# Taking the norm's row scale out of the transposes: weights at the split, roots at the products

## The chip, the cores and the metric

The kernel runs on one core of a Trainium2 chip. The metric is device time in microseconds (us), the median of three runs. One more execution was recorded by the profiler; every row below is from it.

## The reference

512 tokens of 1024 features pass through two blocks. Only the first block is touched. It is, cut to what matters:

```python
def rms_norm(x, g):
    y = x * rsqrt(mean(x * x, axis=-1) + EPS)
    return y * g

h = rms_norm(x, g_mix_norm)
z = h @ w_in        # q, k | v, o | gates | c_q, c_kv | k_pe
...                 # mLSTM heads from q, k, v, o, gates; latent attention from c_q, c_kv, k_pe
x = x + concat(y_a, y_b) @ w_out
h = rms_norm(x, g_ffn_norm)
x = x + square(relu(h @ w_ff1)) @ w_ff2
```

A norm multiplies row t of x by a root r(t), and column k by a weight g(k). r(t) goes through a product with a matrix unchanged, so it may be applied before or after it. The second block (retention, differential attention, PEER) has norms of its own.

## The kernel before

**Tiles.** The tokens are 4 blocks of 128 rows (`tb`). A matrix product contracts over features, so both operands must have features on the partitions: the normed activations are kept transposed, as `xTh` and `xTl` (128 features x 8 feature tiles x 512 tokens). A float32 number is held as a rounded high part and the rest, and one product is three TensorE matmuls (`mm3`, L130 to L132: high by high, high by low, low by high). A weight page of 128x1024 is loaded into one of three buffers `raw`, then split by ScalarE (`Ah`, L105) and VectorE (`Al`, L86; GpSimd for the very first page).

**The norm before.** For each block: ScalarE squares the row and sums it (L164), VectorE adds EPS (`rsqt`, L137), GpSimd takes the power -1/2 (`r`, L138), VectorE forms `hn` = x * r * g (L172; g was loaded as a 512 KB tile `gb` that repeats it on all partitions). TensorE transposes the eight 128x128 tiles of `hn` into two PSUM banks (`ptr`, L156), and for each bank ScalarE writes the high part of all four tiles in one instruction (L159, 128x512) and VectorE the low part in another (L86). Products then come out as the reference has them.

**First use, at the start.** `ws_first` multiplies three pages of `w_in` (gates, then two of the latent pages) by the transposed tokens in two halves of 256 tokens: 3 pages x 8 tiles x 3 matmuls for the first half, the transposes of the last blocks, then the second half. After it come the gate rows (`F7`, transposed to `pf` at L375), the latent vectors `ch`, `cl` and `csq` from the banks `pw` and `pc` (L417 to L420), the q and kv products `puq`, the normed keys `na` (L509) and their transposes `pqt` (L531), the convolution of `pq` (L594 and on) and the v and o products.

**Second use, at the FFN.** `out_last` adds the product with `w_out` to x block by block (`pol`), and takes one step of the norm after each block; then `ws_first` multiplies the first three pages of `w_ff1`. Relu (ScalarE, L734) and square (VectorE, L735) follow on each of 32 such products. While this runs, weight pages of the second block are split ahead (`shl`, ScalarE L117, GpSimd L86) and written to memory.

**Order.** A scheduler writes the instructions of each engine into one queue; an engine takes its queue in order and waits at the first instruction that isn't ready. Loads are issued by SyncE's queue, each waiting for its buffer. At the start a hand-written stretch (`manual_schedule`) gives the order for ScalarE and VectorE.

## Time and profile before

| | |
|---|---|
| median of three runs | 2127.32 us (2127.05 to 2130.56) |
| the profiled execution: its time | 2128.51 us |
| the profiled execution: its span | 2126.7 us |
| TensorE matmuls busy | 2090.7 us (98%) |
| VectorE, ScalarE, GpSimd busy | 1541.3, 858.6, 534.6 us |

A row of the timeline gives the start in us from the span's start, the duration, the engine (PE is TensorE, DVE VectorE, ACT ScalarE, POOL GpSimd, PEld TensorE's weight load), the line, output<-inputs, shapes, and in brackets how long the engine had been idle and what ended that. A row that groups instructions gives their number, busy time, mean ns of one, and the idle time ahead of them. A row of stretches gives busy us (and instructions) for each engine, then the granted TensorE clock as a share of full speed, the DMA engines' busy share and GB/s.

### The profile page before, as it was taken

To read this page: it belongs to the slowest core of one execution; us is meant where nothing else is said; L and a number is where in the kernel's file an instruction comes from. 1 tells how busy PE (TensorE), PEld (TensorE's weight loads), DVE (VectorE), ACT (ScalarE), POOL (GpSimd) and SP (SyncE) were. 2 spreads that over 40 slices of the span, in tenths; PEclk is the share of its full clock that TensorE was granted. 3 is DMA by queue.
4 is the path that set the end of the run, shared out by engine and by line. 5 is a ranking of instruction groups with operands and counts; after the bars stand their busy time and mean duration, and the time that the engine had idled before them with its cause. 6 is when DMAs were issued, how large, how long until landed. Compare 5 with 4: busy or idle time off the path is not lost.

```text
span 2126.7 us, 29751 instructions
## 1 busy us (share of the span) xinstructions
PE 2090.7 (98%) x10985; PEld 1807.7 (85%) x10985; DVE 1541.3 (72%) x3039; ACT 858.6 (40%) x1505; POOL 534.6 (25%) x387
## 2 busy tenths in 40 slices
PE   7999999999999999999999999999999999999998
PEld 6856888888888778888999999999888889899886
DVE  6846666556444763679979799978888878778784
ACT  5645354444324543311335544333333333333332
POOL 1100034444100000100000004544555554444330
PEclk9999999999999999999999999999999999999999
DMA  5210269899512222354898778999999999998981
GB/s 191 68 41 21 90 239 353 318 340 345 205 60 89 69 70 91 108 199 165 278 352 302 280 228 312 372 360 338 319 343 333 351 319 338 330 335 319 322 291 61
DMA packets 178977, 507.55 MB, mean 239 GB/s; under 512 B 15632, under 2 KB 73872, under 8 KB 172048
## 3 DMA queue, kind: packets, MB, share of 16 engines
q1 hardware_dynamic: 136208, 329.47, 45.6%
q0 software_dynamic: 42624, 176.18, 22.0%
...
## 4 chain that ended last, share of the span: by engine, by line
PE 96%; DVE 1%; DMA 1%; ACT 1%; issue 0%; SPq 0%; POOL 0%; DVEq 0%; POOLq 0%; ACTq 0%
PE pA L130 11%; PE pA L131 11%; PE pA L132 11%; PE po L132 8%; PE po L130 8%; PE po L131 8%; PE pO L131 3%; PE pO L132 3%; PE pO L130 3%; PE pts L132 2%; PE pts L130 2%; PE pts L131 2%; PE pGm L1147 2%; PE pQ L130 1%; PE pQ L131 1%; PE pQ L132 1%
## 5 line engine op out<-in xcount | busy, mean ns | idle before, releaser
L130 PE MATMUL pA<-xTh,Ah 128*128 128x384 f32 (+1 forms) x1256 | 434.0, 346 | 0.3 <-ACT ge L1166 0.3
L132 PE MATMUL pA<-xTh,Al 128*128 128x384 f32 (+1 forms) x1256 | 434.2, 346 | 0.0
L131 PE MATMUL pA<-xTl,Ah 128*128 128x384 f32 (+1 forms) x1256 | 434.0, 346 | 0.0
L105 ACT ACTIVATE Ah<-raw 128x1024 fp32r<-128x1024 f32 x203 | 215.1, 1060 | 329.9 <-PE pA L131 228.2
L86 DVE TENSOR_TENSOR Al<-raw,Ah 128x1024 fp32r<-128x1024 f32 x202 | 249.8, 1237 | 122.7 <-ACT Ah L105 119.1
L1236 POOL DMA_INDIRECT gu<-peer_u_rows,eidx x128 | 182.6, 1426 | 581.0 <-issue 394.3
L132 PE MATMUL po<-Bh,Wl 128*128 128x512 f32 x714 | 278.6, 390 | 0.0
L131 PE MATMUL po<-Bl,Wh 128*128 128x512 f32 x714 | 278.2, 390 | 0.0
L131 PEld LDWEIGHTS pA<-xTl,Ah 128*128 128x128 f32 x1256 | 235.9, 188 | 14.3
L130 PEld LDWEIGHTS pA<-xTh,Ah 128*128 128x128 f32 x1256 | 235.8, 188 | 14.1 <-ACT ge L1166 0.6
L132 PEld LDWEIGHTS pA<-xTh,Al 128*128 128x128 f32 x1256 | 235.8, 188 | 12.0
L1236 POOL DMA_INDIRECT gv<-peer_v,eidx x128 | 190.2, 1486 | 197.2 <-DVE acc L1252 180.2
L130 PE MATMUL po<-Bh,Wh 128*128 128x512 f32 x714 | 225.0, 390 | 0.0
L86 DVE TENSOR_TENSOR Bl<-raw,Bh 128x1024 fp32r<-128x1024 f32 x151 | 193.7, 1284 | 19.9 <-ACT Bh L105 19.2
L1297 ACT ACTIVATE Wh<-w 128x384 fp32r<-128x384 f32 x128 | 67.1, 525 | 342.8 <-PE po L131 313.1
L105 ACT ACTIVATE Bh<-raw 128x1024 fp32r<-128x1024 f32 x151 | 157.7, 1049 | 68.2 <-PE pO L132 45.9
L1252 DVE SCALAR_TENSOR_TENSOR acc<-gv,w,acc 128x1024 f32<-128x1024 f32 x128 | 164.0, 1281 | 2.2 <-DMA gv<-peer_v,eidx 2.2
L1242 DVE SCALAR_TENSOR_TENSOR gu<-gu,hn 128x1024 f32<-128x1024 f32 x128 | 155.8, 1219 | 3.8 <-DMA gu<-peer_u_rows,eidx 3.8
L132 PEld LDWEIGHTS po<-Bh,Wl 128*128 128x128 f32 x714 | 134.0, 188 | 26.2
L86 DVE TENSOR_TENSOR Wl<-w,Wh 128x384 fp32r<-128x384 f32 x128 | 71.1, 556 | 117.4 <-ACT Wh L1297 109.5
L131 PEld LDWEIGHTS po<-Bl,Wh 128*128 128x128 f32 x714 | 134.1, 188 | 25.7
L130 PEld LDWEIGHTS po<-Bh,Wh 128*128 128x128 f32 x714 | 133.2, 188 | 22.1
...
## 6 DMA issues: line engine op xcount, KB each, us to landing
raw<-peer_v SPq DMA_DIRECT2D x128, 512.0 KB, 6.4
raw<-peer_u SPq DMA_DIRECT2D x104, 512.0 KB, 6.5
...
raw<-w_ff SPq DMA_DIRECT2D x64, 512.0 KB, 6.2
...
Al<-Sd SPq DMA_DIRECT2D x40, 512.0 KB, 5.9
Ah<-Sd SPq DMA_DIRECT2D x40, 512.0 KB, 5.5
```

The lines of the kernel that those rows point to most:

```text
L86: eng.tensor_tensor(o, a, hi.bitcast(F32), op=OP.subtract)
L105: S.activation(hi, raw, AF.Copy)
L130: PE.matmul(ps, lh, rh, start=start, stop=False)
L131: PE.matmul(ps, lh, rl, start=False, stop=False)
L132: return PE.matmul(ps, ll, rh, start=False, stop=stop)
L1147: PE.matmul(o, hot[:, 0, jp, :, jb], val[:, p, jp, :, jb], start=p == 0, stop=p == 1)
L1236: G.indirect_dma_start(out=r, out_offset=None, in_=rows, in_offset=bass.IndirectOffsetOnAxis(ap=eidx[s // 64][:, s % 64:s % 64 + 1], axis=0))
L1242: V.scalar_tensor_tensor(r, r, 1.0, xn3, op0=OP.mult, op1=OP.mult, accum_out=act3[:, s:s + 1])
L1252: V.scalar_tensor_tensor(acc3, r, w3[:, s:s + 1], acc3, op0=OP.mult, op1=OP.add)
L1297: S.activation(wh, w, AF.Copy)
```

## The change

Both norms of the first block lose `hn` and `gb`. x itself is transposed. The split of the transposed tile multiplies by g, which is now one number per partition and feature tile: ScalarE writes `xTh` = ptr * g and VectorE `xTl` = ptr * g - `xTh`. As g differs from tile to tile, each bank now takes four ScalarE and four VectorE instructions of 128x128 (L170, L171), where it took one of each. The roots of all four blocks are formed on the side, transposed and copied as `rootT` (the root of token t in column t, on all partitions; L193, L194), and applied where the products are read: as a column of scales where tokens are on the partitions (v, o), by a VectorE multiply with `rootT` where they are on the columns (`F7`, the four `pq`, the FFN's products), and as factors of the small root vectors in the latent part. In the FFN the pair Relu on ScalarE, square on VectorE becomes max-and-multiply on VectorE, square on ScalarE. `hn` rows of blocks 2 and 3 no longer lie in the buffers of `wu`; `kg` shares a buffer now.

```diff
+    def put_raw(h, l, src, kt0, n, tb, gT):
+        pt = bank("att", "ptr")
+        for j in range(n):
+            PE.transpose(pt[:, j * P:(j + 1) * P], src[:, j * P:(j + 1) * P], ident)
+        t = slice(tb * P, (tb + 1) * P)
+        for j in range(n):
+            g, ps = gT[:, kt0 + j:kt0 + j + 1], pt[:, j * P:(j + 1) * P]
+            S.activation(h[:, kt0 + j, t], ps, AF.Copy, scale=g)
+            V.scalar_tensor_tensor(l[:, kt0 + j, t], ps, g, h[:, kt0 + j, t].bitcast(F32), op0=OP.mult, op1=OP.subtract)
...
+        def roots(dst):
+            for tb in range(NT):
+                ss = square_sum(tmp.tile([P, D], F32, tag="hn", name="hn", bufs=2), x[tb])
+                rsq(root[:, tb:tb + 1], ss, 1.0 / D, EPS)
+            pt = bank("att", "prt")
+            for tb in range(NT):
+                PE.transpose(pt[:, tb * P:(tb + 1) * P], root[:, tb:tb + 1].to_broadcast([P, P]), ident)
+            S.activation(dst, pt, AF.Copy)
+            return root
...
-        sq[0]()
-        fin[0]()
-        sq[1]()
-        fin[1]()
         turn[0]()
+        turn[1]()
         pgs.append(page(None, G, raw=raws[0]))
-        sq[2]()
-        turn[1]()
         pgs.append(page(None, V, raw=raws[1]))
-        fin[2]()
-        sq[3]()
-        fin[3]()
+        turn[2]()
         pgs.append(page(None, V, raw=raws[2]))
-        turn[2]()
+    rootT = main.tile([P, D], F32, tag="gb", name="rootT", bufs=1)[:, 0:T]
+    root = roots(rootT)
...
-    S.activation(F7, ps, AF.Identity, bias=gbias)
+    V.tensor_tensor(F7, ps, rootT, op=OP.mult)
+    V.tensor_scalar(F7, F7, gbias, None, op0=OP.add)
...
+    for n, (rc, width) in enumerate(((rcq, 256), (rkv, 128))):
+        c = slice(4 * n, 4 * n + 4)
+        V.tensor_tensor(ssc[:, c], ssc[:, c], root2, op=OP.mult)
+        rsq(rc, ssc[:, c], 1.0 / width, EPS)
+        V.tensor_tensor(rc, rc, root, op=OP.mult)
...
         ws_mm(ps, page(wf[i]), h, l)
+        V.tensor_tensor(ps, ps, rootT, op=OP.mult)
...
-        S.activation(v1[:, tb, :, 0:128], ps.rearrange("p (h d) -> p h d", h=4), AF.Copy)
+        S.activation(v1[:, tb, :, 0:128], ps.rearrange("p (h d) -> p h d", h=4), AF.Copy,
+                     scale=root[:, tb:tb + 1])
...
-        S.activation(og[:, tb], ps, AF.Tanh, scale=0.5)
+        S.activation(og[:, tb], ps, AF.Tanh, scale=half_root[:, tb:tb + 1])
...
+    rootT = fp.tile([P, T], F32, name="rootT")
+    roots(rootT)
...
-            S.activation(r, ps, AF.Relu)
-            V.tensor_tensor(r, r, r, op=OP.mult)
+            V.scalar_tensor_tensor(r, ps, 0.0, rootT, op0=OP.max, op1=OP.mult)
+            S.activation(r, r, AF.Square)
```

How the scheduler lays this out is read from the queues of both programs, below. A row is a place in an engine's queue, the line, output<-inputs, the shape and what it waits for (a counter of PE, DVE, Activation or a DMA queue); xN stands for N such rows in a run.

**ScalarE at the start**, from the first norm instruction to the second weight page, before:

```order
3 L164 ACTIVATE hn,ss<-x 128x1024 [waits DMAHW3_49]
4 L159 ACTIVATE xTh<-ptr 128x4x128 [waits PE_49] x2
5 L105 ACTIVATE Ah<-raw 128x1024 [waits DMAHW4_49]
6 L164 ACTIVATE hn,ss<-x 128x1024 [waits DMAHW5_49]
7 L159 ACTIVATE xTh<-ptr 128x4x128 [waits PE_49] x2
8 L105 ACTIVATE Ah<-raw 128x1024 [waits DMAHW6_49]
```

And now (the stretch between two squares and the second weight page; ahead of it stand seven more `xTh` pieces and three squares):

```order
10 L170 ACTIVATE xTh<-ptr,gT 128x128 [waits DVE_49]
11 L170 ACTIVATE xTh<-ptr,gT 128x128 [waits PE_49]
12 L170 ACTIVATE xTh<-ptr,gT 128x128 [waits DVE_49] x3
13 L170 ACTIVATE xTh<-ptr,gT 128x128 [waits PE_49]
14 L170 ACTIVATE xTh<-ptr,gT 128x128 [waits DVE_49]
15 L194 ACTIVATE rootT<-prt 128x512 [waits PE_49]
16 L170 ACTIVATE xTh<-ptr,gT 128x128 [waits DVE_49]
17 L380 ACT_TABLE_LOAD
18 L380 ACTIVATE sin<-red 128x128 [waits DVE_49]
19 L170 ACTIVATE xTh<-ptr,gT 128x128 [waits DVE_49]
20 L105 ACTIVATE Ah<-raw 128x1024 [waits DMAHW4_49]
21 L105 ACTIVATE Ah<-raw 128x1024 [waits DMAHW6_49]
```

The first weight page moved from behind two `xTh` instructions to behind sixteen, four squares, the copy of the roots and the sine with its table load; and only the first piece of a bank waits for TensorE, the other three wait for VectorE.

**VectorE at the same place**, now (`posf`, `ang`, `nn`, `red` form the rotary angles, `gqk` a product of weights; before, `ang` stood behind all four `xTl` of the first two blocks):

```order
12 L171 SCALAR_TENSOR_TENSOR xTl<-ptr,gT,xTh 128x128 [waits Activation_49] x2
13 L330 TENSOR_SCALAR half_root<-root 128x4 [waits Pool_49]
14 L332 TENSOR_TENSOR root_225<-root 128x4
15 L484 TENSOR_TENSOR gqk<-gq_b,gk_b 128x128 [waits DMAHW6_49,DMAHW5_49]
16 L171 SCALAR_TENSOR_TENSOR xTl<-ptr,gT,xTh 128x128 [waits Activation_49]
17 L362 CAST posf<-posi 128x4 [waits DMAHW0_49]
18 L366 TENSOR_SCALAR ang<-invf,posf 128x32 [waits DMAHW1_49,DVE_49]
19 L171 SCALAR_TENSOR_TENSOR xTl<-ptr,gT,xTh 128x128 [waits Activation_49]
20 L366 TENSOR_SCALAR ang<-invf,posf 128x32 x3
21 L171 SCALAR_TENSOR_TENSOR xTl<-ptr,gT,xTh 128x128 [waits Activation_49]
```

Pieces of the second block now stand behind instructions that wait for the loads of `gq_b`, `gk_b`, `posi` and `invf`; ten pieces stand ahead of `posf`.

**TensorE at the end of the latent stage**, the last transposes of the keys' and queries' parts (`na`, `ro`), before:

```order
442 L132 MATMUL pts<-Ah,xTl 128x512
443 L641 MATMUL pM<-MxP,sel 128x512 x2
444 L536 MATMUL pqt<-ident,ro 128x128 x2
445 L531 MATMUL pqt<-ident,na 128x128 x4
446 L536 MATMUL pqt<-ident,ro 128x128 x2
447 L641 MATMUL pM<-MxP,sel 128x512 x2
448 L531 MATMUL pqt<-ident,na 128x128 x4
449 L536 MATMUL pqt<-ident,ro 128x128 x2
```

And now:

```order
436 L131 MATMUL puq<-hk,ch_539 128x512
437 L132 MATMUL puq<-hk,cl_540 128x512
438 L559 MATMUL pqt<-ident,na 128x128 x4
439 L671 MATMUL pM<-MxP,sel 128x512 x2
440 L564 MATMUL pqt<-ident,ro 128x128 x2
441 L559 MATMUL pqt<-ident,na 128x128 x4
442 L564 MATMUL pqt<-ident,ro 128x128 x2
443 L559 MATMUL pqt<-ident,na 128x128 x4
444 L564 MATMUL pqt<-ident,ro 128x128 x2
```

The products `pts` that stood between the last `puq` and these transposes now stand ahead of the last `puq`, and the first `na` follows it directly.

**ScalarE at the entry of the FFN**, before:

```order
252 L164 ACTIVATE hn,ss<-x 128x1024
253 L159 ACTIVATE xTh<-ptr 128x4x128 x2
254 L117 ACTIVATE shl<-sraw 128x1024
255 L105 ACTIVATE Bh<-raw 128x1024 x2
256 L159 ACTIVATE xTh<-ptr 128x4x128 x2
```

And now:

```order
271 L201 ACTIVATE hn,ss<-x 128x1024
272 L117 ACTIVATE shl<-sraw 128x1024
273 L170 ACTIVATE xTh<-ptr,gT 128x128 x3
274 L117 ACTIVATE shl<-sraw 128x1024
275 L105 ACTIVATE Bh<-raw 128x1024
276 L170 ACTIVATE xTh<-ptr,gT 128x128 x2
277 L105 ACTIVATE Bh<-raw 128x1024
278 L170 ACTIVATE xTh<-ptr,gT 128x128 x6
279 L105 ACTIVATE Bh<-raw 128x1024
280 L170 ACTIVATE xTh<-ptr,gT 128x128 x2
281 L194 ACTIVATE rootT<-prt 128x512
```

The pieces of the last blocks are spread between page splits (`Bh`) and splits ahead (`shl`).

## Rows read from the trace of the kernel before

**Rows 1.** The page: busy us, share of the span and instructions of each engine.
```profile
PE 2090.7 (98%) x10985; PEld 1807.7 (85%) x10985; DVE 1541.3 (72%) x3039; ACT 858.6 (40%) x1505; POOL 534.6 (25%) x387
```

**Rows 2.** Stretches (us): busy us of each engine, granted clock, DMA share, GB/s.
```profile
0.00:13.40 13.40, 3.70 (x16) 3.14 (x16) 4.31 (x10) 7.25 (x11) 4.22 (x10) 1.00 0.85 316
...
44.00:56.00 12.00, 10.15 (x43) 9.04 (x43) 10.29 (x17) 4.28 (x11) 0.00 (x0) 0.72 0.29 89
...
60.00:80.00 20.00, 20.00 (x98) 16.78 (x98) 19.27 (x48) 16.10 (x45) 3.61 (x4) 1.00 0.24 79
...
292.00:296.00 4.00, 2.47 (x11) 2.26 (x11) 4.00 (x4) 1.09 (x2) 0.88 (x2) 0.52 1.02 420
...
640.00:2126.70 1486.70, 1474.04 (x8030) 1309.48 (x8028) 1159.24 (x2368) 559.28 (x950) 385.86 (x273) 1.00 0.74 260
```

**Rows 3.** Timeline of the start: start, duration, engine, instruction, idle time before it.
```profile
4.31 1.06 ACT L164 ACTIVATE hn<-x 128x1024 f32<-128x1024 f32 x1 [2.28 <-DMA x<-x]
...
8.31 1.97 PE L156 MATMUL ptr<-ident,hn 128*128 128x128 f32 x8 [8.31 <-DVE hn L172]
...
10.81 1.05 ACT L105 ACTIVATE Ah<-raw 128x1024 fp32r<-128x1024 f32 x1
...
11.94 2.37 POOL L86 TENSOR_TENSOR Al<-raw,Ah 128x1024 fp32r<-128x1024 f32 x1 [1.64 <-ACT Ah L105]
...
16.04 0.28 PE L131 MATMUL pw<-xTl,Ah 128*128 128x256 f32 x1
...
16.16 0.28 PE L132 MATMUL pw<-xTh,Al 128*128 128x256 f32 x1
...
20.70 0.68 DVE L342 TENSOR_SCALAR ang<-invf,posf 128x32 f32<-128x32 f32 x4 [2.07 <-DMA invf<-c_invf]
...
36.45 0.60 PE L375 MATMUL pf<-ident,F 128*128 128x128 f32 x4
```

**Rows 4.** Groups of ScalarE and VectorE: count, busy us, mean ns, idle before.
```profile
L687 ACT ACTIVATE hf<-pH,dn 128x128 f32<-128x128 f32 x16 | 5.6, 361 | 8.3 <-DVE dn L685 6.2 <-DVE dn L683 1.7 <-DVE dn L684 0.4
...
L688 DVE SCALAR_TENSOR_TENSOR hs<-pH,dn,hf 128x128 f32<-128x128 f32 x16 | 5.5, 345 | 2.1 <-ACT hf L687 1.9
...
L1166 ACT ACT_TABLE_LOAD x6 | 7.7, 1283 | 0.1
...
L668 DVE SCALAR_TENSOR_TENSOR E<-pS,E 128x512 f32<-128x512 f32 x8 | 5.5, 688 | 1.0 <-PE pS L653 0.5 <-ACT E L667 0.5
```

**Rows 5.** Timeline at 45 to 48 us, VectorE, ScalarE and TensorE.
```profile
45.93 0.75 DVE L418 SCALAR_TENSOR_TENSOR cl<-pw,gcq,ch 128x512 fp32r<-128x512 f32 x1
...
46.71 0.60 ACT L420 ACTIVATE csq<-pw 128x512 f32<-128x512 f32 x1 [1.73 <-DVE cl L418]
...
47.36 1.44 PE L426 MATMUL prc<-ones,csq 128*128 128x1 f32 x6 [1.85 <-ACT csq L420]
```

**Rows 6.** DMA issues up to 60 us: count, KB, median us to landing.
```profile
raw<-w_uq SPq DMA_DIRECT2D x2, 512.0 KB, 6.3
```

**Rows 7.** Timeline of the latent stage's end, GpSimd and TensorE.
```profile
112.99 1.01 POOL L138 TENSOR_TENSOR rqk<-rsqt,nhalf 128x4 f32<-128x4 f32 x1 [6.43 <-DVE rsqt L137]
...
115.34 0.63 PE L531 MATMUL pqt<-ident,na 128*128 128x128 f32 x4 [1.43 <-DVE na L509]
```

**Rows 8.** Timeline of the FFN's entry, VectorE, GpSimd, ScalarE, TensorE.
```profile
289.21 4.18 DVE L172 SCALAR_TENSOR_TENSOR hn<-x,r,gb 128x1024 f32<-128x1024 f32 x1 [0.17 <-POOL r L138]
...
289.92 2.37 POOL L86 TENSOR_TENSOR shl<-sraw,shl 128x1024 fp32r<-128x1024 f32 x1
...
286.09 1.04 ACT L164 ACTIVATE hn<-x 128x1024 f32<-128x1024 f32 x1
...
293.53 0.87 PE L156 MATMUL ptr<-ident,hn 128*128 128x128 f32 x3 [3.51 <-DVE hn L172]
...
305.86 0.40 PE L130 MATMUL pA<-xTh,Ah 128*128 128x512 f32 x1
```

More of the change, by code (lines that the diff above doesn't have):

```diff
@@ L160, in put_T, with raw_T, turn, step @@
         sub(V, l[:, kt0:kt0 + n, tb * P:(tb + 1) * P], psv, dst)
+    def put_raw(h, l, src, kt0, n, tb, gT):
[7 more added lines that the diff above has]
+            V.scalar_tensor_tensor(l[:, kt0 + j, t], ps, g, h[:, kt0 + j, t].bitcast(F32), op0=OP.mult, op1=OP.subtract)
+    def raw_T(x, gname, lag=1):
+        gT = main.tile([P, KT], F32, tag="gT", name="gT", bufs=2)
+        nc.sync.dma_start(gT, I[gname])
+        h, l = new_xT()
+        root = main.tile([P, NT], F32, tag="root", name="root", bufs=2)
+        def turn(tb):
+            for half in range(2):
+                put_raw(h, l, x[tb][:, half * 512:(half + 1) * 512], half * 4, 4, tb, gT)
+        def step(tb):
+            if tb >= lag:
+                turn(tb - lag)
+        def roots(dst):
[7 more added lines that the diff above has]
+            return root
+        return h, l, roots, step, [lambda tb=tb: turn(tb) for tb in range(NT)]
     def square_sum(o, xt):
@@ L172, in norm_rows, with norm_T @@
         return V.scalar_tensor_tensor(o, xt, r, gb, op0=OP.mult, op1=OP.mult)
-    def norm_T(x, gname, room=None, lag=1):
+    def norm_T(x, gname, lag=1):
         gb = bcast_row(I[gname], D, "gb")
@@ L192, in step @@
                 done.append(norm_rows(rows[tb], x[tb], gb))
-        if room is None:
-            return h, l, rows, step, [lambda tb=tb: turn(tb) for tb in range(NT - lag, NT)]
-        for tb in range(NT):
-            rows[tb] = room(tb)
-        sums = {}
-        order = [lambda tb=tb: sums.update({tb: square_sum(rows[tb], x[tb])}) for tb in range(NT)]
-        rest = [lambda tb=tb: norm_rows(rows[tb], x[tb], gb, sums[tb]) for tb in range(NT)]
-        turns = [lambda tb=tb: turn(tb) for tb in range(NT)]
-        return h, l, order, rest, turns
+        return h, l, rows, step, [lambda tb=tb: turn(tb) for tb in range(NT - lag, NT)]
     def ws_mm(ps, pg, h, l, n=T):
@@ L279, in body @@
     x = new_x()
+    nc.sync.dma_start(ident, I["c_ident"])
     load_x(x, 0)
-    h, l, sq, fin, turn = norm_T(
-        x, "g_mix_norm",
-        lambda tb: tmp.tile([P, D], F32, tag="hn", name="hn", bufs=2) if tb < 2 else
-        m1.tile([P, 2, D], F32, tag="yb", name="hn", bufs=2)[:, 0])
-    nc.sync.dma_start(ident, I["c_ident"])
+    h, l, roots, _, turn = raw_T(x, "g_mix_norm")
     load_x(x, 1)
@@ L294, in body @@
     with tc.manual_schedule(engines={mybir.EngineType.Activation, mybir.EngineType.DVE}):
-        sq[0]()
-        fin[0]()
-        sq[1]()
-        fin[1]()
         turn[0]()
+        turn[1]()
         pgs.append(page(None, G, raw=raws[0]))
-        sq[2]()
-        turn[1]()
         pgs.append(page(None, V, raw=raws[1]))
-        fin[2]()
-        sq[3]()
-        fin[3]()
+        turn[2]()
         pgs.append(page(None, V, raw=raws[2]))
-        turn[2]()
+    rootT = main.tile([P, D], F32, tag="gb", name="rootT", bufs=1)[:, 0:T]
+    root = roots(rootT)
+    half_root = m1.tile([P, NT], F32, name="half_root")
+    V.tensor_scalar(half_root, root, 0.5, None, op0=OP.mult)
+    root2 = m1.tile([P, NT], F32, name="root2")
+    V.tensor_tensor(root2, root, root, op=OP.mult)
     R = 36
@@ L461, in body @@
         S.activation(sq[:, 0:64], kflat[:, tb], AF.Square, accum_out=ssp[:, tb:tb + 1])
-    kg = lp.tile([P, NT, 64], F32, name="kg")
+    kg = lp.tile([P, NT, 64], F32, tag="ra", name="kg", bufs=1)
     V.tensor_tensor(kg, kflat, gk_b[:, None, 128:192].to_broadcast([P, NT, 64]), op=OP.mult)
@@ L712, in body @@
         sub(V, yl[:, hd, :], pt, yh[:, hd, :])
-    h, l, _, norm, norm_end = norm_T(x, "g_ffn_norm")
+    h, l, roots, norm, norm_end = raw_T(x, "g_ffn_norm")
+    norm_end = norm_end[NT - 1:]
     out_last(x, I["w_out"], yh, yl, lambda: ma.tile([P, T], F32R, tag=f"E{T}", name="X", bufs=4), norm)
@@ L1369, in pack @@
     A["positions"] = np.ascontiguousarray(f("positions").reshape(NT, P).T)
-    for n in ("g_mix_norm", "g_mlstm_out", "g_q", "g_k", "g_ffn_norm"):
+    for n in ("g_mlstm_out", "g_q", "g_k"):
         A[n] = sq(n)
+    for n in ("g_mix_norm", "g_ffn_norm"):
+        A[n] = np.ascontiguousarray(sq(n).reshape(KT, P).T)
     w = sq("w_in")
```

2 lines of the change are left out of this document (removed).

## The prediction

> **What bounds the kernel now.** First the page's busy line: TensorE works in 2090.7 of 2126.7 us [rows 1]. So work taken from the other engines is worth nothing in itself; the time moves where TensorE waits, or by what TensorE is given to do, and that hardly changes (8 transposes of roots more). Next the stretches: from 640 us to the end TensorE is busy in 1474 of 1487 us at full clock [rows 2], the queues there are the same in both kernels, and a delay brought in from before 640 finds nothing to soak it up. All is decided earlier. There the stretches and the timeline show the places where TensorE stands still and the change has a hand: the first 13.4 us, where it is busy for 3.70 [rows 2], 44 to 56 us, the end of the latent stage at 115 us, and the entry of the FFN at 290 us. I take them in turn, as differences at TensorE's next fixed point; a shift of an earlier point is handed on in full since TensorE has no slack in between.
>
> **The pairs.** A bank's split was one ScalarE and one VectorE instruction on 128x512 and is now four of each on 128x128. In the queue each ScalarE piece but the first of a bank waits for a count that VectorE's piece before it in that bank raises, and VectorE's waits for ScalarE's. So in one bank the two take turns. The nearest rows are a pair of the mLSTM stage with the same forms, a 128x128 PSUM read with a scale column on ScalarE, 361 ns, and a 128x128 VectorE instruction of three operands reading the same PSUM tile, 345 ns [rows 4]. The handoff: ScalarE's `csq` began at 46.71, having waited 1.73 us for VectorE's `cl`, which ends at 45.93 + 0.75 = 46.68 [rows 5], so 0.03 us. A pair takes 0.36 + 0.35 + 0.06 = 0.77 us, a block of eight 6.2. `csq` and `cl` both only read the bank `pw` and still stand one behind the other: reads of a bank by two engines are kept apart in this program.
>
> The Trainium skill, PSUM — Partial Sum Buffer, section PSUM bank collisions raise a hardware error, speaks against this change: it says two engines may not be in the same bank and partition quadrant at once, two reads included, and that software has to keep them apart. By that rule the pairs take turns as `csq` and `cl` do, and the sum stays as below; were overlapping allowed, it would be the faster rival's.
>
> **1. The start.** Before, x lands at 4.31, the norm chain lets the first transposes go at 8.31, page 0 is split at 10.81 (`Ah`), and GpSimd's low part is done at 11.94 + 2.37 = 14.31; from then `ws_first` runs, and the next work, `pf`, starts at 36.45 [rows 3]. Now the transposes need x alone. They may go at 4.3, some 4 us earlier, and the first piece at 4.8. But ScalarE has, ahead of `Ah`, 16 pieces, four squares, the copy of the roots, a table load and the sine. By pairs that is 16 x 0.77 = 12.3; squares 4 x 1.06 = 4.2 [rows 3]; copy 0.6 (as `csq`, same shape from PSUM [rows 5]); table load 1.28; sine 0.36 as a 128x128 row [rows 4]. 4.8 + 12.3 + 4.2 + 2.2 = 23.5; where squares fit in ScalarE's waits of 0.4 a pair, 1.6 less, 21.9. VectorE adds a wait: its pieces from the eleventh on stand behind `ang`, which waits for `invf`. Before it began at 20.70 after 2.07 us of waiting [rows 3]. Of the loads issued ahead of it one of 512 KB (`gb`) is gone, 1.2 us at the highest rate among the stretches, 420 GB/s [rows 2], so `invf` is there at about 19.5. Six pairs (4.6) and 2.2 behind that give 26.3. Between 21.9 and 26.3 I take 25.4, near the upper end, since the load's row speaks for it. Then `Ah` 1.05 and the low part 2.37: 28.9, against 14.31.
>
> From there 144 matmuls of 256 columns at 0.12 us (starts 16.04, 16.16 [rows 3]) are 17.3, and eight transposes between them, none longer than that, 0.9: `pf` at 47.1. It will hardly be 47.1: the three `raw` buffers are free only once the pages are split, at 26 to 29, the loads behind them need 6.3 [rows 6], and their splits (`wu`, `hk`) stand in ScalarE's queue ahead of the last block's pieces. That takes some 2.4: `pf` at 49.5, **+13**. Bounds: with 21.9 and none of this, 25.3 + 18.2 = 43.5, +7; with one whole landing of 6.3 on top of 47.1, +17.
>
> **2. End of the latent stage.** The transposes of `na` waited 1.43 us for VectorE at 115.34; behind the last `puq` there are ScalarE's sums, `rsqt`, GpSimd's power (112.99, 1.01 us) and `na` [rows 7]. From the power's start to the transposes that is 2.35; the four sums at 0.36 as ScalarE's 128x128 [rows 4] make 1.4, `rsqt` and handoffs some 0.5: 4.3 in all. It was covered by `pts` matmuls that stood between; now these stand ahead of the last `puq`, and all of the chain shows: 4.3 instead of 1.4, +3, and 1 for the low clock that followed other waits of this length (granted 0.52 after the 3.51 us at 290 [rows 2, 8]). The four multiplies of `pq` by `rootT` and two for `F7` (0.69 each, as a 128x512 VectorE instruction on PSUM [rows 4]) fall in a stage where VectorE is busy 19.27 of 20 us, yet TensorE 20.00 [rows 2]: nothing in the middle, 4 x 0.69 = 2.8 at most. **+4**, 0 to 6.
>
> **3. 44 to 56 us.** `prc` waits 1.85 for `csq` [rows 5], and over these 12 us TensorE is busy for 10.15 at a granted clock of 0.72 [rows 2]: 1.85 of wait and, as an estimate, 0.28 x 10.15 = 2.85 of slow matmuls behind it, 4.7 lost. With TensorE 13 later than VectorE's scans (which read `pf`, so only partly) the wait may go: **-2**, -4.7 to 0.
>
> **4. Entry of the FFN.** Before, the last `hn` took 4.18 us (289.21) where GpSimd's split took 2.37 beside it, TensorE idled 3.51, the clock was 0.52, and the first wide products began at 305.86 [rows 2, 8]. That `hn` is gone. The last square began at 286.09 [rows 8]. In the new queue there are behind it 13 pieces, three `Bh` and two `shl` of 1.05 each, with the square 6.3. Pieces of two banks alternate there, so a piece costs 0.36 to 0.77: 4.7 to 10. The last piece is done between 297.1 and 302.4. Its feature tile is the last of each page: two pages of 24 matmuls, 5.8, follow, giving 302.9 to 308.2 against 305.86. **+1**, in bounds of -6 (idle time and low clock both gone) to +6 (a `shl` held up by its store as well).
>
> The Trainium skill, SBUF — State Buffer, section Who interferes with whom, has VectorE and GpSimd share one pair of ports under an exclusive lock. The 4.18 us beside GpSimd's split [rows 8] agree; by this alone place 4 would be worth -3, as the new pieces read PSUM for one operand.
>
> **Costed at nothing.** The relu: ScalarE's relu and VectorE's square become VectorE 0.69 [rows 4] and a ScalarE square, in series as before, under 24 matmuls of 512 columns, 48 x 0.12 = 5.8 a page; uncovered, under 1 us once. Scale columns of v and o: an operand instead of a number, eight instructions. Small VectorE instructions in the latent roots: six on 128x4, each under the 0.35 of a 128x128 [rows 4], and needed only where `puq` is read; at most 2. `gb`'s traffic: counted in 1.
>
> **Sum.** 13 + 4 - 2 + 1 = +16. The profiled execution took 2128.5; this makes 2144.5, and the median, 1.2 lower, 2127.3 + 16 = **2143**.
>
> **Rivals.** (a) *Slower still*: the weight pages land late and both chains show in full, 17 + 6 + 0 + 4 = +27, 2154. For it: three buffers freed late, 6.3 a landing. Against: nothing else loads then (DMA 0.85 busy before in that time [rows 2], with 512 KB more). (b) *Given back*: the start costs its lower bound, and the stalls of 3 and 4 vanish: 7 + 4 - 4.7 - 6 = 0, 2127 to 2128. For it: both stalls hang on chains through `hn` or VectorE that are shorter or gone. Against: ScalarE's queue at 4 is longer than before. (c) *Faster*: the pieces do not take turns but run side by side, so that 16 cost 16 x 0.36 = 5.8; `Ah` follows at 4.8 + 5.8 + 4.2 + 2.2 = 17.0, low part at 20.4, `pf` at 20.4 + 18.2 = 38.6, +2; the shorter entry of the FFN gives its 6, place 3 its 4.7: -8.7, 2119. It decides at the wait inside a bank: below 0.45 us a piece this wins, provided `invf` comes by 14. For it: each engine alone needs only 0.36. Against: the counts in the queue, and `csq`. That the change does not do what it says (transposes still held by the norm) I leave out: no root stands ahead of them.
>
> **How the numbers follow.** A difference of 0.2%, 4.3 us, is about what a measurement of this kernel tells from none. Forecast 0.67 (its own range 2135 to 2151), (a) 0.16, (b) 0.10, (c) 0.07. The range runs from 2134, the forecast with the start at +7 and a little, to 2155, above (a): (b), (c) and a rest lie outside. Faster 0.07, same 0.10, slower 0.83.
>
> **What would show it.** In the profile after: L170 and L171 taking turns at 0.77 a pair; page 0's `Ah` near 25 and the first steady matmuls near 29; `pf` near 49; a wait of 4 to 5 us ahead of the last `na` transposes; no `hn` wait at the FFN, but waits for `xTh` or `xTl` pieces. Wrong would be: pieces at 0.4 us, `Ah` before 18, or TensorE's idle time growing after 640 us.

## The result, and the profile after

Five runs have a median of 2160.73 us (2155.66 to 2166.14) against 2127.05 (2122.46 to 2130.56, five runs of before): slower, by a ratio of 1.0168 (95% interval 1.0153 to 1.0184). The forecast was 2143, in a range up to 2155: the direction was right, the size was half of what came. The profiled execution took 2166.14 us, its span is 2164.3.

First the page's busy line and three stretches (busy us of PE, PEld, DVE, ACT, POOL, then granted clock, DMA share, GB/s):

```profile
PE 2112.7 (98%) x10993; PEld 1818.5 (84%) x10993; DVE 1541.6 (71%) x3091; ACT 871.9 (40%) x1554; POOL 533.8 (25%) x387
...
0.00:29.00 29.00, 10.14 (x40) 7.77 (x41) 12.59 (x44) 16.03 (x34) 6.29 (x13) 0.72 0.48 156
...
29.00:50.00 21.00, 19.11 (x131) 18.40 (x130) 9.50 (x19) 9.09 (x18) 0.00 (x0) 0.82 0.42 144
...
640.00:2164.00 1524.00, 1511.26 (x8160) 1338.03 (x8158) 1174.77 (x2389) 567.58 (x964) 386.51 (x276) 1.00 0.73 255
```

The busy line answers [rows 1]: TensorE is *busy* for 22 us more, with eight short matmuls more to do. From 640 us on it is again busy nearly all the time, as in [rows 2], and its idle time there hasn't grown (12.7 us in both), but the stretch to the end is 1524 us, not 1487. As 640 us is another place in the program now, a fairer measure follows below. The first 50 us have a granted clock of 0.72 and 0.82.

The start, on the timeline (start, duration, engine, instruction, idle time before it and what ended it):

```profile
9.12 0.37 ACT L170 ACTIVATE xTh<-ptr,gT 128x128 fp32r<-128x128 f32 x1 [0.42 <-DVE xTl L171]
...
9.52 0.35 DVE L171 SCALAR_TENSOR_TENSOR xTl<-ptr,gT,xTh 128x128 fp32r<-128x128 f32 x1 [0.43 <-ACT xTh L170]
...
9.90 0.63 ACT L170 ACTIVATE xTh<-ptr,gT 128x128 fp32r<-128x128 f32 x2 [0.42 <-DVE xTl L171]
...
17.42 0.24 DVE L366 TENSOR_SCALAR ang<-invf,posf 128x32 f32<-128x32 f32 x1 [0.53 <-DMA invf<-c_invf]
...
22.61 2.00 ACT L105 ACTIVATE Ah<-raw 128x1024 fp32r<-128x1024 f32 x2
...
23.70 0.58 PE L130 MATMUL pw<-xTh,Ah 128*128 128x256 f32 x1 [3.77 <-ACT Ah L105]
...
27.22 0.58 PE L132 MATMUL pw<-xTh,Al 128*128 128x256 f32 x1 [1.77 <-DVE Al L86]
...
27.00:33.00 6.00, 5.78 (x27) 5.78 (x28) 2.44 (x8) 2.98 (x7) 0.00 (x0) 0.50 0.46 175
...
39.81 1.06 ACT L105 ACTIVATE wu<-raw 128x1024 fp32r<-128x1024 f32 x1 [3.31 <-DMA raw<-w_uq]
...
41.18 0.62 PE L130 MATMUL pw<-xTh,Ah 128*128 128x256 f32 x3 [1.19 <-ACT xTh L170]
...
42.45 0.39 PE L131 MATMUL pw<-xTl,Ah 128*128 128x256 f32 x1 [0.65 <-DVE xTl L171]
...
51.85 0.60 PE L400 MATMUL pf<-ident,F 128*128 128x128 f32 x4
```

(The line that begins with 27.00:33.00 is a stretch.) A piece of ScalarE (9.12), the piece of VectorE (9.52), ScalarE again (9.90): one pair takes 0.78 us, and each engine waits 0.42 us in it. Behind waits of 3.77 and 1.77 us TensorE's products run at the lower of its two clock levels, granted 0.50, 1.2 GHz: 27 of them take 5.78 us from 27 to 33 us, where 0.12 each [rows 3] would make 3.2. At 39.81 ScalarE's split `wu` had waited 3.31 for its load; the last block's pieces stand behind it, and TensorE waits 1.19 and 0.65 for them. `ang` began at 17.42 (20.70 in [rows 3]), both pages' `Ah` at 22.61 (10.81), the first product at 23.70, `pf` at 51.85 (36.45).

The end of the latent stage, where [rows 7] stood:

```profile
127.26 1.01 POOL L138 TENSOR_TENSOR rqk<-rsqt,nhalf 128x4 f32<-128x4 f32 x1 [5.73 <-DVE rsqt L137]
...
129.60 1.09 PE L559 MATMUL pqt<-ident,na 128*128 128x128 f32 x4 [4.60 <-DVE na L537]
...
131.76 3.62 PE L584 MATMUL psc<-kT,qT 128*128 128x512 f32 x4
...
135.32 2.04 PE L585 MATMUL psc<-kT,qT 64*128 64x512 f32 x4
...
129.60:135.30 5.70, 5.70 (x14) 3.18 (x14) 0.00 (x0) 1.39 (x5) 0.00 (x0) 0.50 0.00 0
```

In before the same scores are:

```profile
116.46 1.97 PE L556 MATMUL psc<-kT,qT 128*128 128x512 f32 x4
...
118.36 1.98 PE L557 MATMUL psc<-kT,qT 64*128 64x512 f32 x4
```

4.60 us of waiting for `na`, and up to 135.3 us a granted clock of 0.50, 1.2 GHz: the first four scores take 3.62 us, not 1.97. The four behind them are back to before's time (2.04 and 1.98).

The entry of the FFN, where [rows 8] stood:

```profile
307.51 2.39 POOL L86 TENSOR_TENSOR shl<-sraw,shl 128x1024 fp32r<-128x1024 f32 x1
...
307.53 3.45 DVE L86 TENSOR_TENSOR Bl<-raw,Bh 128x1024 fp32r<-128x1024 f32 x1 [1.82 <-ACT Bh L105]
...
311.01 0.33 SPq L93 DMA_DIRECT2D raw<-w_ff  x1
...
319.39 1.06 ACT L105 ACTIVATE Bh<-raw 128x1024 fp32r<-128x1024 f32 x1 [5.83 <-DMA raw<-w_ff]
...
320.76 1.01 PE L130 MATMUL pw<-xTh,Ah 128*128 128x256 f32 x3 [3.77 <-ACT xTh L170]
...
330.07 0.39 PE L130 MATMUL pA<-xTh,Ah 128*128 128x512 f32 x1
```

VectorE's `Bl` began 0.02 us behind GpSimd's split and took 3.45. At its end, 310.98, a page buffer is free and SyncE issues the next load (311.01). ScalarE's `Bh` waits 5.83 for its load of `w_ff`; behind it in the queue stand the last `xTh` pieces, and TensorE waits 3.77 for them. The wide products begin at 330.07 (305.86).

How far TensorE is behind before at fixed points of its queue shows where the time goes. Each number is the start of the first matmul with that output, less the start in the first trace of before (kernels other than after are explained below):

| first | before, us | before again | after | two_banks | after_align | mix_align | ffn_align | before_pad |
|---|---|---|---|---|---|---|---|---|
| `pf` | 36.45 | -0.6 | +15.4 | +7.2 | +13.1 | +13.3 | -2.0 | -1.3 |
| `pM` | 111.88 | -3.2 | +8.4 | +0.1 | +5.5 | +5.7 | -2.3 | -3.8 |
| `pov` | 126.50 | -4.5 | +17.2 | +9.0 | +15.2 | +14.3 | -2.2 | -5.1 |
| `pol` | 256.05 | -4.4 | +18.0 | +9.9 | +17.7 | +15.1 | -2.2 | -4.8 |
| `pA` of the FFN | 305.86 | -6.0 | +24.2 | +9.1 | +16.6 | +14.2 | -4.5 | -4.9 |
| `pDS` | 666.58 | -6.0 | +27.9 | +12.9 | +16.9 | +14.2 | -3.7 | -1.4 |
| `po` | 1232.27 | -5.4 | +30.9 | +16.2 | +16.8 | +14.9 | -4.0 | +3.4 |
| last matmul | 2116.05 | -5.4 | +37.5 | +22.9 | +16.8 | +14.9 | -4.0 | +12.0 |

The table settles two things. The second trace of before is 5 us ahead of the first: one execution of equal queues can differ from another by that much. And after loses 13 us between `pA` and the last matmul; 10 of them from `pDS` on, where TensorE's queue is the same, instruction by instruction, as in before. That last stretch, first in before, then in after:

```profile
666.58:2116.05 1449.47, 1447.77 (x7841) 1285.46 (x7840) 1142.53 (x2340) 546.45 (x928) 384.76 (x271) 1.00 0.75 265
...
694.45:2153.57 1459.12, 1457.12 (x7841) 1291.15 (x7840) 1142.93 (x2340) 546.47 (x928) 383.76 (x271) 1.00 0.75 263
```

The same 7841 matmuls at full clock, 1.7 and 2.0 us of idle time, and 9.4 us more of busy time: the loss is no wait.

### The profile page after: what moved, and what is told of

It reads as the page before. It is cut to its first block, busy times and chain, and to the rows that moved or that the text cites. A ratio compares the mean times of both kernels' runs of the same rounds, so it can differ in the third digit from the quotient of the medians.

```text
span 2164.3 us, 29901 instructions
## 1 busy us (share of the span) xinstructions
PE 2112.7 (98%) x10993; PEld 1818.5 (84%) x10993; DVE 1541.6 (71%) x3091; ACT 871.9 (40%) x1554; POOL 533.8 (25%) x387
## 4 chain that ended last, share of the span: by engine, by line
PE 94%; DMA 2%; ACT 1%; DVE 1%; issue 0%; SPq 0%; POOL 0%; DVEq 0%; POOLq 0%; ACTq 0%
PE pA L131 11%; PE pA L132 11%; PE pA L130 11%; PE po L130 8%; PE po L132 8%; PE po L131 8%; PE pO L131 3%; PE pO L132 3%; PE pO L130 3%; PE pts L130 2%; PE pts L132 2%; PE pts L131 2%; PE pGm L1180 2%; PE pQ L131 1%; PE pQ L132 1%; PE pQ L130 1%
## 5 line engine op out<-in xcount | busy, mean ns | idle before, releaser
L131 PEld LDWEIGHTS pA<-xTl,Ah 128*128 128x128 f32 x1256 | 235.7, 188 | 15.4
```

The source lines that it names most:

```text
L131: PE.matmul(ps, lh, rl, start=False, stop=False)
```

## The experiments

Medians (us), each beside the median of before that was measured together with it, and the ratio with its 95% interval:

| kernel | this | before | ratio |
|---|---|---|---|
| after_again | 2159.75 | 2124.81 | 1.0158 (1.0141 to 1.0175) |
| mix_only | 2156.91 | 2124.81 | 1.0148 (1.0131 to 1.0165) |
| ffn_only | 2147.01 | 2124.81 | 1.0099 (1.0079 to 1.0119) |
| two_banks | 2151.20 | 2124.81 | 1.0133 (1.0112 to 1.0155) |
| before_pad | 2142.02 | 2126.12 | 1.0083 (1.0065 to 1.0101) |
| after_pad | 2153.39 | 2126.12 | 1.0140 (1.0119 to 1.0160) |
| wide_pages | 2152.73 | 2126.12 | 1.0128 (1.0110 to 1.0146) |
| before_pad256 | 2126.36 | 2124.77 | 1.0008 (0.9996 to 1.0020) |
| before_pad96 | 2134.75 | 2124.77 | 1.0049 (1.0033 to 1.0066) |
| before_front96 | 2125.68 | 2124.77 | 1.0000 (0.9988 to 1.0013) |
| two_banks_pad | 2146.87 | 2124.77 | 1.0099 (1.0071 to 1.0128) |
| after_align | 2141.48 | 2125.05 | 1.0082 (1.0065 to 1.0099) |
| after_align_late | 2140.70 | 2125.05 | 1.0081 (1.0064 to 1.0098) |
| before_late | 2123.36 | 2125.05 | 0.9990 (0.9978 to 1.0003) |
| two_align_late | 2135.80 | 2125.05 | 1.0062 (1.0043 to 1.0082) |
| mix_align | 2143.28 | 2126.70 | 1.0079 (1.0053 to 1.0105) |
| ffn_align | 2125.50 | 2126.70 | 0.9995 (0.9979 to 1.0010) |

### The same again, one norm alone, and banks by turns

My first theory: the queues cost some 26 us (the table has 24.2 at `pA`), and the rest is the pace of one slow execution.

**after_again** is the changed kernel, unedited.

> The changed kernel once more, for a second trace. Theory: of its 34 us, what lies before the first FFN product (26 us in the first trace) is in the order of the queues and comes back within 2 us; the further 10 us that the first trace collects between 640 us and the end, with no idle time on TensorE, are the pace of that one execution (it took 2166, the others 2156 to 2162). So the span from the first pts of the second block to the end is within 3 us of before's here. Rival: the slower pace belongs to the changed kernel (its tiles lie elsewhere), and the same 10 us are there again.

It was 2159.75, and its trace has the same 10 us from `pDS` to the end (+28.5 to +38.0). The pace belongs to the kernel; the first theory fell on this point.

**mix_only** and **ffn_only** each keep one norm's part of the change.

```diff
-    h, l, roots, norm, norm_end = raw_T(x, "g_ffn_norm")
-    norm_end = norm_end[NT - 1:]
+    h, l, _, norm, norm_end = norm_T(x, "g_ffn_norm")
...
-            V.scalar_tensor_tensor(r, ps, 0.0, rootT, op0=OP.max, op1=OP.mult)
-            S.activation(r, r, AF.Square)
+            S.activation(r, ps, AF.Relu)
+            V.tensor_tensor(r, r, r, op=OP.mult)
```

(mix_only; ffn_only is the kernel before with these lines the other way round, and `kg` sharing its buffer.)

> Only the first norm is changed; the FFN's norm, its relu and square are as before. Theory: start and latent stage keep their cost, the first pol comes 18 us after before's, the FFN's entry is as before: 16 to 20 us slower than before in all. Rival (the cost sits at the FFN, the start is given back): under 10 us slower.

> Only the FFN's norm is changed. Theory: the last pieces stand in ScalarE's queue behind a page split that waits for its load, so TensorE stands still for some 7 us in the entry where it stood 3.5 before, with the low clock after it: 6 to 10 us slower than before. Rival (this part is neutral by itself and was late only because the first part had shifted the loads): within 3 us of before.

32 and 22 us slower, both well above what I expected, and 54 together where the whole change costs 34. So something of about 15 to 20 us comes with *either* part and is counted twice. What the two have in common is not an instruction of the late stages, but the small tiles `gT` and `root`: 128 bytes per partition that move all later tiles. That they are the cause is still a guess here; it is tried below.

**two_banks** transposes a block into both banks first and issues the pieces by turns.

```diff
-            for half in range(2):
-                put_raw(h, l, x[tb][:, half * 512:(half + 1) * 512], half * 4, 4, tb, gT)
+            pts = [bank("att", "ptr") for _ in range(2)]
+            for k in range(KT):
+                PE.transpose(pts[k // 4][:, k % 4 * P:(k % 4 + 1) * P], x[tb][:, k * P:(k + 1) * P], ident)
+            for k in (0, 4, 1, 5, 2, 6, 3, 7):
+                g, ps = gT[:, k:k + 1], pts[k // 4][:, k % 4 * P:(k % 4 + 1) * P]
+                S.activation(h[:, k, t], ps, AF.Copy, scale=g)
+                V.scalar_tensor_tensor(l[:, k, t], ps, g, h[:, k, t].bitcast(F32), op0=OP.mult, op1=OP.subtract)
```

> Both banks of a block are transposed first and their pieces issued alternately, so that ScalarE works in one bank while VectorE works in the other; everything else as in the changed kernel. Theory (pairs taking turns set the start): a piece costs some 0.4 us instead of 0.78, the first page is split about 5 us earlier, and the time is 5 to 8 us below the changed kernel's. Rival (page order and loads set the start, not the pairs): within 2 us of the changed kernel.

ScalarE's timeline, and TensorE's first steady product:

```profile
9.78 0.62 ACT L186 ACTIVATE xTh<-ptr,gT 128x128 fp32r<-128x128 f32 x2 [0.16 <-DVE xTl L187]
...
10.57 0.37 ACT L186 ACTIVATE xTh<-ptr,gT 128x128 fp32r<-128x128 f32 x1 [0.16 <-DVE xTl L187]
...
16.02 2.00 ACT L105 ACTIVATE Ah<-raw 128x1024 fp32r<-128x1024 f32 x2
...
21.69 0.58 PE L132 MATMUL pw<-xTh,Al 128*128 128x256 f32 x1 [2.82 <-DVE Al L86]
```

Two pieces now start 0.79 us apart from the next two, 0.4 each; the waits are 0.16. `Ah` follows at 16.02 instead of 22.61 and `pf` is 8 us earlier (table), about half of the start's cost; the median falls by 8.6. Not all of this is the pairs: the queue changed too, and the sine with its table load, the copy of the roots and two pieces, 2.9 us of ScalarE in after, now stand behind `Ah`. This run can't separate the two.

### The place of the tiles

**before_pad**, **before_pad256**, **before_pad96** are the kernel before with an unused tile behind the transposed activations (and `kg` sharing a buffer for room; in the built programs the queues differ from before's by the pad's `memset` alone); **before_front96** has 96 bytes ahead of everything instead.

```diff
+    pad = main.tile([P, 32], F32, tag="pad", name="pad", bufs=1)
+    V.memset(pad, 0.0)
     load_x(x, 1)
```

> The kernel before once more, for a second trace, to see what pace its matmuls have here. Theory (placement: the change adds small tiles ahead of the weight pages and moves every later tile by 128 bytes per partition, and matmuls read them more slowly there): the 128x384 matmuls of the last stage start 0.1735 us apart as in the first trace, not 0.1762 as in the four changed kernels. Rival (pace is a matter of the execution): 0.176 here too.

> The kernel before with an unused tile of 128 bytes per partition behind the transposed activations, so that all later tiles lie where the changed kernel has them, and kg sharing a buffer to make room. Theory (placement): the last stage's 128x384 matmuls start 0.176 us apart, and from 640 us to the end it loses about 8 to 10 us; 8 to 14 slower than before in all. Rival (pace comes with the new instructions, not with the place): 0.1735 apart, within 3 us of before.

> As before_pad, with 256 bytes instead of 128: the queues of the two are the same, and the weight pages lie, counted within 256 bytes, where the kernel before has them. Theory (placement, by position within 256 bytes): 128x384 matmuls 0.1747 us apart, about 17 us below before_pad, so within 4 us of before. Rival (any shift or the memset costs it): as before_pad, 2142.

> As before_pad, with 96 bytes: raw, Ah and Al then start at a multiple of 256. If only a distance of 128 counts, something between before_pad and before_pad256; if a start at a multiple of 256 is best, 128x384 matmuls under 0.1747 us apart and a time at or below before's; if it is worst, above 0.177 and over 2142. No theory of mine says which; I lean to at or below before's.

> The kernel before with 96 bytes ahead of everything, so that x, xTh, xTl, raw, Ah and Al all start at multiples of 256. If the starts themselves count: faster than before_pad96. If it is the weight pages alone: as before_pad96.

The three pads have the same queues and differ in bytes alone: 2142.0 with 128, 2134.8 with 96, 2126.4 with 256. With 96 ahead of all tiles the time is that of before (2125.7); I had leaned to "at or below" for 96 as well, and that was wrong. Groups of TensorE by form (count, busy us, mean ns of one; a matmul's duration overlaps the next one's, so these are not to be summed), first before_pad, then before_pad256, then before_pad96:

```profile
L130 PE MATMUL pA<-xTh,Ah 128*128 128x384 f32 x1024 | 346.9, 339 | 0.0
...
L130 PE MATMUL pA<-xTh,Ah 128*128 128x512 f32 x232 | 91.6, 395 | 0.0
```

```profile
L130 PE MATMUL pA<-xTh,Ah 128*128 128x384 f32 x1024 | 343.5, 335 | 0.3 <-ACT ge L1168 0.3
...
L130 PE MATMUL pA<-xTh,Ah 128*128 128x512 f32 x232 | 90.5, 390 | 0.0
```

```profile
L130 PE MATMUL pA<-xTh,Ah 128*128 128x384 f32 x1024 | 345.0, 337 | 0.0
...
L130 PE MATMUL pA<-xTh,Ah 128*128 128x512 f32 x232 | 91.9, 396 | 0.0
```

339 against 335 ns in the 128x384 form; with 96 bytes that form is at 337 and the 512 form at 396. The distance from start to start (us, the mean over each trace of TensorE's timeline, waits left out) gives the size: 0.1768 - 0.1746 = 0.0022 for 3072 matmuls of the 384 form is 6.8 us of the 16. By the same count 696 `pA` of 512 columns give 3.3, 672 `pts` 2.0 and 2304 `po` 4.1, together 16.2. (The 384 form's mean takes in some 35 longer gaps in every kernel; the last stage alone, which the expectations speak of, has 0.1735 in before and 0.1758 in before_pad.) The table has it beside where the pages `Ah` start relative to `xTh` in the built programs (bytes, counted within 256):

| kernel | `xTh` at | `Ah` at | apart | `pA` 384 | `pA` 512 | `pts` 512 | `po` 512 |
|---|---|---|---|---|---|---|---|
| before, before_again | 160 | 160 | 0 | 0.1747 | 0.2276 | 0.2291 | 0.2278 |
| before_pad256, ffn_align | 160 | 160 | 0 | 0.1746 | 0.2276 | 0.2291 | 0.2278 |
| before_front96 | 0 | 0 | 0 | 0.1746 | 0.2276 | 0.2289 | 0.2278 |
| before_pad96 | 160 | 0 | 96 | 0.1747 | 0.2342 | 0.2326 | 0.2282 |
| before_pad, ffn_only | 160 | 32 | 128 | 0.1768 | 0.2323 | 0.2321 | 0.2296 |
| after, two_banks, mix_only | 224 | 32 | 64 | 0.1765 to 0.1768 | 0.2334 | 0.2307 | 0.2283 |
| after_pad | 224 | 160 | 192 | 0.1744 | 0.2290 | 0.2332 | 0.2290 |
| after_align, mix_align | 224 | 224 | 0 | 0.1747 | 0.2276 | 0.2298 | 0.2278 |

**after_pad** puts 128 bytes more into the changed kernel, **after_align** 192, so that the two operands are a multiple of 256 apart.

> The changed kernel with the same 128 bytes more, so that weight pages lie 256 bytes from where before has them. Theory (placement by position within 256 bytes): the last stage is back at 0.1735 us, and the time 8 to 12 us below the changed kernel's, about 2149. Rival (place doesn't matter, or by another measure): within 3 us of the changed kernel.

> The changed kernel with 192 bytes more, so that weight pages and transposed activations are a multiple of 256 bytes apart, as in before (in after_pad they are 64 off). Theory (it is the distance of the two operands within 256 bytes): all forms at before's pace, 128x512 pts 0.229 where after_pad had 0.233, pA 0.2276 where it had 0.229, so 3 to 6 us below after_pad from 311 us on, 2147 to 2151 in all; what is left over before is the order of the queues alone. Rival (the distance is not it): pace as in after_pad or after, 2153 to 2160.

after_pad gained 6.4 us against after_again, less than I expected: one form is at its old pace, `pts` is slower than ever. after_align gained 18.3, more than I expected, to **16.4 us over before**, and in the table of fixed points it stays at 16.8 from `pDS` to the end. Its groups, beneath those of after:

```profile
L130 PE MATMUL pA<-xTh,Ah 128*128 128x384 f32 x1024 | 346.0, 338 | 0.0
...
L130 PE MATMUL pA<-xTh,Ah 128*128 128x512 f32 x232 | 91.8, 396 | 0.0
```

```profile
L130 PE MATMUL pA<-xTh,Ah 128*128 128x384 f32 x1024 | 343.5, 335 | 0.2 <-ACT ge L1201 0.2
...
L130 PE MATMUL pA<-xTh,Ah 128*128 128x512 f32 x232 | 90.6, 391 | 0.1
```

All kernels with the operands a multiple of 256 bytes apart run at the old pace (`pts` of after_align within 0.3%); all others are slower in at least two of the first three forms. A start at 0 is slow in before_pad96 and fast in before_front96, so it is not the position of the page alone. Nor is it, in the 512 form, other engines at work: in before_pad, the 59 `pA` 512 beside which VectorE, ScalarE and GpSimd all stood still are 0.2325 apart, the others 0.2323 (in before 50 such are at 0.2280); the 10 of them beside which no DMA ran either are 0.2331 apart (in before 0.2289). More than that isn't shown. Other tiles move too; `po` loses some of its pace although its own operands (`Bh`, `Wh`) keep their distance in all these kernels, so that distance isn't the whole; and why the 384 form does not follow the 512 form stays open.

### The FFN's entry, and the parts without the pace

**after_align_late**, **before_late** and **two_align_late** hold the splits ahead back until the relu of their page is done.

```diff
-            S.activation(wh, r, AF.Copy)
+            made = S.activation(wh, r, AF.Copy)
...
-            for n in range(split, (i + 1) * AHEAD // 32):
-                split_ahead(n, fp)
+            with tc.issue_after(ins(made)):
+                for n in range(split, (i + 1) * AHEAD // 32):
+                    split_ahead(n, fp)
```

> after_align with the splits ahead of the second block held back until the relu of their FFN page is done; nothing is left out. Theory (at the FFN's entry GpSimd's split and VectorE's Bl shut each other out, the next load of w_ff is late, and ScalarE's last pieces stand behind a Bh that waits for it): that Bh waits under 1 us, the entry costs 0 to 2 us where the first trace showed 8: 3 to 8 us below after_align. Rival (pieces in one bank alone make it late): within 2 us of after_align.

> The kernel before with the same splits held back. Theory (the last hn takes 4.2 us beside GpSimd's split and 1.3 alone): TensorE's wait of 3.5 at the FFN's entry falls to about 1: 2 to 5 us faster than before. Rival (the splits cost as much later, where ScalarE and VectorE have less room): within 2 us, or slower.

> Alternate banks, placement as before, and splits held back: the three causes taken away. Theory (they add up): the start costs 7 and the latent stage's end 6 less the 5 of a stall that goes, the rest nothing: 2130 to 2137. Rival (another cause is left): over 2140.

after_align_late: 2140.7 against 2141.5, nothing. The reason stands in the trace of after_align, on VectorE, GpSimd, SyncE and ScalarE:

```profile
307.27 1.23 DVE L86 TENSOR_TENSOR Bl<-raw,Bh 128x1024 fp32r<-128x1024 f32 x1 [1.55 <-ACT Bh L105]
...
307.52 3.18 POOL L86 TENSOR_TENSOR shl<-sraw,shl 128x1024 fp32r<-128x1024 f32 x1
...
308.52 0.33 SPq L93 DMA_DIRECT2D raw<-w_ff  x1
...
313.30 1.06 ACT L105 ACTIVATE Bh<-raw 128x1024 fp32r<-128x1024 f32 x1 [0.58 <-DMA raw<-w_ff]
```

Here `Bl` began 0.25 us *ahead* of GpSimd's split. It took 1.23 and the split 3.18, the buffer came free earlier (load issued at 308.52, not 311.01), and `Bh` waited 0.58 where it had waited 5.83. The load, too, was quicker, 4.8 us from issue to `Bh` against 8.4; why isn't shown. The entry then costs nothing: -1.1 from `pol` to `pA` in the table, +6.2 in after. after, after_again, ffn_only and two_banks_pad have the one outcome (+6.0 to +6.3), after_pad, after_align and two_banks the other (-0.8 to -1.1); in after_pad `Bl` was 0.03 us ahead. That holds for the traced executions. The four times of two_banks_pad lie at 2143.0 and 2143.4 and at 2150.4 (the traced one, costly) and 2150.6, so executions of one kernel may well fall either way; no second trace shows it. In any case the traced base had lost what the experiment was to take away. The Trainium skill, SBUF — State Buffer, section Who interferes with whom, tells of one pair of ports that VectorE and GpSimd lock against each other; the two outcomes here, 3.45 beside 2.39 and 1.23 beside 3.18, agree with a lock that the earlier one holds. [rows 8] does not fit that alone: there `hn` began at 289.21, 0.71 us *ahead* of the split, and still ended 1.1 us behind its end. What GpSimd had begun just before `hn` is the issue of a store:

```profile
289.13 0.77 POOL L119 DMA_DIRECT2D Sd<-shl  x1
```

Whether that counts as the earlier one isn't shown.

before_late brings the last `hn` back to its price alone:

```profile
285.22 1.27 DVE L172 SCALAR_TENSOR_TENSOR hn<-x,r,gb 128x1024 f32<-128x1024 f32 x1
...
290.11 0.62 PE L130 MATMUL pw<-xTh,Ah 128*128 128x256 f32 x3 [0.40 <-ACT xTh L159]
...
291.49 0.39 PE L131 MATMUL pw<-xTl,Ah 128*128 128x256 f32 x1 [0.76 <-DVE xTl L86]
```

1.27 us, not 4.18 [rows 8], and TensorE is 4.8 us further ahead at `pA` (-1.2 to -6.0); but 2.5 of it is lost again by `pDS`, and the time is the same within what can be measured. two_align_late is 2135.8, within 2130 to 2137 as expected: no further cause of size is needed.

**two_banks_pad** and **wide_pages** came before the distance was known. wide_pages multiplies a whole bank by g on VectorE into SBUF and splits from there, 128x512 each, with the page splits ahead of the second block.

```diff
+        xg = tmp.tile([P, D], F32, tag="hn", name="hn", bufs=2)[:, 0:n * P].rearrange("p (k t) -> p k t", t=P)
+        V.tensor_tensor(xg, pt[:, :n * P].rearrange("p (k t) -> p k t", t=P), gT[:, kt0:kt0 + n, None].to_broadcast([P, n, P]), op=OP.mult)
+        S.activation(h[:, kt0:kt0 + n, t], xg, AF.Copy)
+        sub(V, l[:, kt0:kt0 + n, t], xg, h[:, kt0:kt0 + n, t])
```

> two_banks with 128 bytes more, as after_pad: both causes found so far are taken away. Theory (pairs in a bank, and placement, add up): 7 to 10 us below two_banks, 2141 to 2145; what is left over before is some 9 us of the start and the latent stage's end. Rival (two_banks had no part in it): 2151.

> The weights enter in one VectorE multiply of a whole bank (128x512) into SBUF, from which ScalarE copies the high and VectorE subtracts the low part, 128x512 each; and page splits stand ahead of the second block's turn. Theory (small pieces in one bank make the start late): the first products start before 13.5 us and ws_first ends earlier than in the kernel before; the start costs nothing, and what is left is the end of the latent stage, 4 to 7, and the pace, 8 to 10: 8 to 17 slower than before. Rival (the roots behind the transposes delay F7 and the latent part by as much): 25 or more slower.

two_banks_pad: 2146.9, 2 to 6 over what I expected; the pad left 192 bytes of distance (as in after_pad), and the entry fell the costly way in the traced execution. wide_pages: 27 us slower, as the rival has it, but only in part by the rival's mechanism: at the fixed points it is 4.2 late at `pf`, 9.0 at `pol`, 11.3 at `pA` and 25.0 at the end, so 13.7 are pace (its operands lie 64 apart, as in after). Its first product comes 1.7 us earlier than in before, but then TensorE's own queue holds the roots' transposes between the halves:

```profile
13.56 0.58 PE L131 MATMUL pw<-xTl,Ah 128*128 128x256 f32 x1 [1.27 <-DVE xTl L86]
...
25.05 0.33 PE L193 MATMUL prt<-ident,root 128*128 128x128 f32 x1 [1.52 <-POOL root L138]
...
27.57 0.47 PE L193 MATMUL prt<-ident,root 128*128 128x128 f32 x1 [1.32 <-POOL root L138]
```

Every one of the four transposes of roots waits for GpSimd (two are shown).

**mix_align** and **ffn_align** are mix_only and ffn_only with the distance of before.

> mix_only with the pages placed as in after_align, so that the first norm's change is timed without the pace. Theory: mix_only less some 14 us, the order's cost of the first norm alone, 14 to 18 slower than before, 2139 to 2143; 128x384 matmuls 0.1747 apart. Rival (the first norm's part was slower for another reason): 2150 or more.

> ffn_only with the pages a multiple of 256 bytes from the transposed activations. Theory: ffn_only less some 14 us, the FFN's part alone: 0 to 8 slower than before, by how the fourth Bh falls. With mix_align it should make 16 to 24, against after_align's 16. Rival: 2140 or more.

16.6 slower and 1.2 faster (ratio 0.9995, interval 0.9979 to 1.0010: no difference). Together 15.4, and after_align has 16.4: without the pace the parts add up within the noise, and all of the queues' cost that can be measured is the first norm's.

## Why the prediction was right, and where it was wrong

The direction and the cost of the queues came out; the step that failed is the one that put everything from 640 us on at 0.

**The pairs.** 0.77 us predicted, 0.78 measured (9.12 to 9.90). Right; two_banks, where a piece costs 0.4, is 8.6 us faster, part of it by its changed queue.

**The start, +13.** `pf` came 15.4 late in the first trace, 13.1 in after_align, 12.7 in after_pad. Near, but two terms inside were off and cancel: `invf` came at 17.4 and not 19.5, so `Ah` began at 22.6 and not 25.4; and the products behind it ran at 1.2 GHz up to 33 us (5.8 us where the sum has 3.2), which the sum left out. The 2.4 set aside for late pages was 1.8, and by the mechanism named (`wu` ahead of the last block's pieces). The second trace of the changed kernel is 16.2 late at `pf` and its products are as far apart there (0.21 us), though its rows grant them 1.00: this clock reading is not one to lean on by itself.

**End of the latent stage +4, 44 to 56 us -2.** The shift went from +15.4 (`pf`) to +8.4 (`pM`) and then to +17.2 (`pov`). The stall of `prc` went, and some matmuls moved behind `pM`; the wait for `na`, predicted 4.3, was 4.60, and its low clock was worth 2.7, not 1 (from `na` to the end of the first four scores 5.7 us, in before 3.0). Net +1.8 against +2. The mechanism was right; that the net is right is luck, as the two sizes were each too small.

**FFN's entry, +1, bounds -6 to +6.** +6.2 in the trace of after, -1.1 in after_align. The spread was seen, the cause wasn't: I let 13 pieces and five splits run through without a wait for a load, and named `Bh` only as busy time. It was the wait for the load of one `Bh`, in one of two outcomes.

**From 640 us, 0.** This is the step that failed: "finds nothing to soak it up" and "handed on in full" were right for waits, and I took equal queues to mean equal time. The sign that I had named, idle time growing after 640 us, did not come, as the loss is busy time. TensorE lost 9.7 us from `pDS` to the end and 3.7 between `pA` and `pDS` without more waiting, because the matmuls themselves are slower at the new place of the tiles. after_align has 0 and 0.3 there. By the medians the pad of after_align is worth 18.3 us of the 34 (after_again 2159.75 to after_align 2141.48). The traces of after and after_align are 20.7 apart at the end: 13.3 of it is pace, and most of the rest is the entry's costlier outcome (7.3), which can't be put down to the placement. What is left is 16.4, where the sum of queues had said 16. So close an agreement is partly luck: the start and the latent stage come out by errors that cancel, and the entry's -1.1 for +1 is made up by 2.5 between `pov` and `pol` that stand in no term.

**Costed at nothing.** ffn_align shows the relu's exchange, with all of the FFN's part, at no difference. The scale columns, the small instructions and the four multiplies of `pq` were not tried alone.

**The rivals.** (c) fell with the 0.78. (b) fell: neither the start came at its lower bound nor did all stalls vanish. (a) came nearest in time, 2154, but not by its mechanism: the page that landed late, `wu`'s, cost TensorE 1.8 us of waiting, which the forecast had in its sum. Two sums have slips that decide nothing: 25.4 + 1.05 + 2.37 is 28.8, not 28.9, and (c) leaves out the +4 of place 2 without a reason.

No version here beats the kernel before by more than can be measured.
